# Sixteen more tokens by row gathers instead of dense experts, and squares of finished rows in SBUF

## Chip, core and metric

One core of a Trainium2 chip runs the whole program. The metric is device time in microseconds (us) of one execution; the kernel before takes 3629.07 us (median of three runs, 3625.85 to 3631.55). Engines are named as in the profile: PE is TensorE's matrix products and PEld its weight loads, DVE is VectorE, ACT is ScalarE, POOL is GpSimd, SP is SyncE, which issues most DMAs.

## What is computed

A decoder block on 512 tokens of width 2048 in float32: convolution and attention mixers (`w_in`, `w_mix`, `w_out`), then an expert layer. Each token chooses, for 8 heads, 16 of 16384 experts (a row of `u` and a row of `v` each), so 128 experts per token:

```
top_s, top_i = lax.top_k(scores, 16)            # per half of the key
sel_s, sel_pos = lax.top_k(cand_s, 16)          # of the 16 x 16 sums
gate = softmax(sel_s)
hidden = einsum("td,thkd->thk", x, u_table[sel_i])
act = gelu(hidden) * gate
out = einsum("thk,thkd->td", act, v_table[sel_i])
return rmsnorm(x + out, norm_final)
```

## The kernel before

The expert layer is done in two ways at once. Tokens 0 to 191 (`G0 = P + NG2`, NG2 = 64, lines 32 and 33) go by row gathers: an indirect DMA on POOL's queue fetches one expert row of 8 KB for each of 128 partitions (line 685, in `gather_tile`), and DVE multiplies it with the token (line 696, a sum per partition) or adds it, weighted, to the token's result (line 703). The other `ND` = 320 tokens go dense: PE multiplies them with all 16384 experts (`dense`), and planes of gates, zero for experts that a token did not choose, mask the activations (line 774).

A gather run keeps 128 partitions full. The first run has 128 tokens with 128 slots each (128 gathers of `u`, then 128 of `v`). The second has 64 tokens on two partition groups, each with 64 of the slots (64 and 64 gathers). At its end the second group's partial sums are moved over with a DMA and added (lines 757 and 758, in `finish`); then `finish_rows` (line 722) squares the rows on ACT for their norm (`rms_scale`, line 189, which writes the squares to a z tile in PSUM, line 193), scales them and stores them.

The dense part has 128 tiles of 128 experts in 16 chunks of 8. `up` makes 48 products per tile (16 blocks of the width, three products each, lines 164 to 166, since a float32 weight is split into a high part, line 133, and a low part, line 134). `down` makes as many for each pair of 128 output columns. So a unit is always 48 products of 128 x 128 weights with ND columns, and it reads 1 MB of weights in two halves (`whalf`, line 142, issue on line 148). There are 256 units: the ups of chunks 0 to 7 (units 0 to 63, while the routing of the later tokens and the gate planes are made beside them), the downs of chunks 0 to 7 (64 to 127), and then up and down of each chunk in turn. The activations of the first eight chunks go to memory without gates (`hdd`, line 800) and come back (`hb`, line 813); the gate planes come back from `gd` as `gt` (line 769). The tokens' products with z tiles in PSUM are added to `dacc` (line 838); in the last down the results are transposed (line 843), added to the residual (line 845), normalized and stored.

The order of each engine's instructions is fixed before the run from a simulated timeline. Gathers are called for by `pump`, once or more per unit: at fixed rates in the mixers and up to unit 59, afterwards at the rate that spreads what is left (`rounds`, line 904) over the units up to 246, times 0.9 below unit 128 (lines 1036 to 1039). A gather is held back by a dependency on a product's output of that time; its consumers on DVE stay in program order. Rows have 4 buffers of 1 MB. What is left of the gathers and the finish is called for between the last up and the last down (`"last"`).

Of the kernel before, what the change touches and what calls it, by code (L numbers as in the profile page):

```python
# [18 lines left out]
P = 128  # L19
# [12 lines left out]
NG2 = 64  # L32
# [48 lines left out]
def block_kernel(ctx, tc, a, out, dbg=None):  # L81
# [77 lines left out]
    def behind(ins):  # L159
        """Queue ins on its engine behind the latest weight product."""  # L160
        tc.add_manual_dep(ins.ins, pe_last[0].ins.name, mybir.DependencyInfo(mybir.DependencyClass.NoSync, mybir.DependencyReason.DATA), reason="behind")
# [27 lines left out]
    def rms_scale(pool, x):  # L189
        ss = pool.tile([P, 2], F32, name="ss", bufs=2)  # L190
        for c in range(2):
            junk = ztile()
            nc.scalar.activation(junk, x[:, c * 1024:c * 1024 + 1024], AF.Square, accum_out=ss[:, c:c + 1])  # L193
        return rms_inv(ss)

    def rms_inv(ss):
        nc.vector.tensor_tensor(ss[:, 0:1], ss[:, 0:1], ss[:, 1:2], OP.add)
        nc.scalar.activation(ss[:, 0:1], ss[:, 0:1], AF.Sqrt, scale=1.0 / D, bias=epst)
# [3 lines left out]
    def turn(x2, k, pin):  # L202
        """Two 128-column blocks of the pair of row tiles, transposed: [128, 2, 256]."""
# [9 lines left out]
    def load_x(h):  # L213
        """Transposed tokens of one half times the norm's gains, split; 1 / rms of each token to inv."""
# [46 lines left out]
    def mixer(h, st, x):  # L261
        """Attention, convolution and their gated merge for one half of the tokens; the merge goes to
        md, and the last of it straight to the tiles of the output projection."""
# [157 lines left out]
    def suffix(pool, z, sp, seg, nj, W):  # L421
        """z minus the sums of sp over the keys from each key to the end."""
# [22 lines left out]
    def outproj(pool, h, m, box):  # L445
        """Output projection and residual of 256 tokens."""
# [38 lines left out]
    def chain(pool, h, box, nhi, nlo, c0):  # L485
        """Normalized, transposed and split tokens of one half from column c0; tokens 0.. to xn2d."""
# [35 lines left out]
    def queries(pool, h, st, nhi, nlo, c0):  # L522
        """Product-key scores of 256 tokens, queued for the top 16 of each group."""
# [25 lines left out]
    def route(pool, tile_no, st):  # L549
        """Product-key routing of one 128-token tile: expert halves and gate of each slot."""  # L550
# [12 lines left out]
        # Of the 16 x 16 sums of two sorted lists only those with (a + 1) * (b + 1) <= 16 can be among  # L563
        # the first 16; rows a of widths 16, 8, 4, 1 hold them all, in the order of the full list.
# [16 lines left out]
        # Position in the compact list -> row a and column b.  # L581
# [52 lines left out]
    def gates(pool, eg, p0, b0, nb):  # L634
        """Dense gate planes of 16-token blocks b0.. from tokens on partitions p0.. of a routing tile."""
# [40 lines left out]
    def gather_tile(pool, np_, nslot, idx, gate, load_x, load_acc, finish):  # L676
        """Row gathers for np_ partitions of (token, slot group), nslot slots each."""
# [50 lines left out]
    def gather(routes):  # L728
        idx = routes[0][0]
        yield from gather_tile(  # L730
            late[1], P, P, idx, st["gate"],
            lambda t: nc.sync.dma_start(t, xn2d[0:P]),
            lambda t: nc.sync.dma_start(t, x2d[0:P]),
            lambda t: finish_rows(t, slice(0, P), final_gain()))
        if not NG2:
            return
        S = P // (P // NG2)
        idx, eg = routes[1]
        idx2 = late[1].tile([P, S], I32, name="idx2")
        gate2 = late[1].tile([P, S], F32, name="gate2")  # L740
        for r in range(P // NG2):
            ps_, ss = slice(r * NG2, r * NG2 + NG2), slice(r * S, r * S + S)
            nc.sync.dma_start(idx2[ps_], idx[0:NG2, ss])
            nc.sync.dma_start(gate2[ps_], eg[0:NG2, 2, ss])

        def load_x(t):
            for r in range(P // NG2):
                nc.sync.dma_start(t[r * NG2:r * NG2 + NG2], xn2d[P:G0])
# [339 lines left out]
```

## Time and profile before

| | us |
|---|---|
| median of the runs | 3629.07 |
| span of the profiled execution | 3629.1 |
| PE busy in it | 3535.7 |
| DVE busy | 2833.4 |
| ACT busy | 1621.6 |
| POOL busy | 644.8 |

The profiled execution's own time is its span; nothing of it lies outside, and it stands at the median of the runs. The page's rows of 40 slices show PE at 8 or 9 tenths in all of them and DVE at 5 to 9 tenths; the DMA engines are at 5 or 6 tenths in the first quarter, in which no gathers run, and at 7 to 9 tenths until the last slice. The core moved 1056.10 MB, 402.68 MB of it by the gathers' queue (q0) and 649.38 MB by SP's (q1).

### The profile page before, as it was taken

Reading aid. Unit: us, or ns where it says so; the run is one execution under the profiler, and the core shown is the slowest. Engines: PE = TensorE matmul, PEld = TensorE weight load, DVE = VectorE, ACT = ScalarE, POOL = GpSimd, SP = SyncE. Lnnn points to the kernel's source line nnn. Section 1 sums busy time; section 2 is a strip of 40 time slices with the busy share of each in tenths; the row PEclk is TensorE's granted clock in tenths of the full one; section 3 lists DMA queues with packets and bytes.
Section 4 is the critical chain, followed back from the end, with each engine's and each line's share of the span. In section 5 each row is a group of like instructions: output and inputs, shape, how many; then the busy total and the mean of one; then the engine's idle time right before and its main releaser. Section 6 shows DMA issues by size and latency. Waiting matters only on the chain.

```text
span 3629.1 us, 63343 instructions
## 1 busy us (share of the span) xinstructions
PE 3535.7 (97%) x25347; PEld 3420.6 (94%) x25347; DVE 2833.4 (78%) x4022; ACT 1621.6 (45%) x2277; POOL 644.8 (18%) x520
## 2 busy tenths in 40 slices
PE   9999999999999999889999999999999999999998
PEld 8999999798888999779999999999999999999997
DVE  6555557558988888788999886888887888888885
ACT  5444445445545543554337773333333333333334
POOL 0000000000234222012121111221122322322220
PEclk9999999999999999999999999999999999999998
DMA  5556666663788899899889889899988988889884
GB/s 194 170 176 219 214 216 216 198 193 127 267 306 332 335 344 356 313 331 344 295 324 334 309 317 364 326 358 337 341 328 327 358 328 336 325 338 349 326 319 150
DMA packets 297815, 1056.10 MB, mean 291 GB/s; under 512 B 36464, under 2 KB 109296, under 8 KB 243568
## 3 DMA queue, kind: packets, MB, share of 16 engines
q1 hardware_dynamic: 242224, 649.38, 51.3%
q0 software_dynamic: 55296, 402.68, 28.9%
q8 instruction: 199, 3.26, 0.3%
q14 instruction: 96, 0.79, 0.1%
HBM read 999.98 MB, written 51.38 MB: 290 GB/s over the span
## 4 chain that ended last, share of the span: by engine, by line
PE 73%; DVE 3%; DMA 2%; issue 2%; ACT 1%; POOL 0%; SPq 0%; DVEq 0%; ACTq 0%; POOLq 0%
PE pj L166 13%; PE pj L164 13%; PE pj L165 13%; PE z L164 9%; PE z L165 9%; PE z L166 9%; PE pj L668 2%; DVE wlo L134 1%; PE z L434 1%; PE tr L416 1%; DVE row L696 1%; DMA wraw<-in_w_mix 1%; DMA row<-in_u,idx 1%; PE z L397 0%; DMA gt<-gd 0%
## 5 line engine op out<-in xcount | busy, mean ns | idle before, releaser
L133 ACT ACTIVATE whi<-wraw 128x1024 fp32r<-128x1024 f32 x827 | 874.2, 1059 | 1229.3 <-PE pj L165 726.4
L134 DVE TENSOR_TENSOR wlo<-wraw,whi 128x1024 fp32r<-128x1024 f32 x827 | 1009.2, 1224 | 415.3 <-ACT whi L133 409.5
L166 PE MATMUL pj<-xhi,wlo 128*128 128x256 f32 x2560 | 719.7, 282 | 11.3 <-DVE wlo L134 11.1
L164 PE MATMUL pj<-xhi,whi 128*128 128x256 f32 x2560 | 721.6, 282 | 6.7 <-ACT whi L133 4.7
L165 PE MATMUL pj<-xlo,whi 128*128 128x256 f32 x2560 | 720.5, 282 | 0.0
L164 PE MATMUL pj<-dxhi,whi 128*128 128x320 f32 (+1 forms) x2304 | 710.0, 308 | 2.8 <-ACT whi L133 2.6
L166 PE MATMUL pj<-dxhi,wlo 128*128 128x320 f32 (+1 forms) x2304 | 704.1, 307 | 4.5 <-DVE wlo L134 4.5
L165 PE MATMUL pj<-dxlo,whi 128*128 128x320 f32 (+1 forms) x2304 | 705.8, 307 | 0.0
L164 PE MATMUL z<-ahi,whi 128*128 128x320 f32 x2048 | 631.0, 309 | 4.0 <-ACT z L193 2.9
L165 PE MATMUL z<-alo,whi 128*128 128x320 f32 x2048 | 631.5, 309 | 2.4 <-DVE alo L134 2.4
L166 PE MATMUL z<-ahi,wlo 128*128 128x320 f32 x2048 | 629.6, 309 | 1.8 <-DVE wlo L134 1.8
L166 PEld LDWEIGHTS pj<-xhi,wlo 128*128 128x128 f32 x2560 | 480.0, 188 | 21.5 <-DVE wlo L134 16.1
L164 PEld LDWEIGHTS pj<-xhi,whi 128*128 128x128 f32 x2560 | 481.7, 188 | 12.6 <-ACT whi L133 6.1
L165 PEld LDWEIGHTS pj<-xlo,whi 128*128 128x128 f32 x2560 | 481.4, 188 | 6.7 <-issue 5.3
L685 POOL DMA_INDIRECT row<-in_v,idx x192 | 286.7, 1493 | 1063.8 <-DVE row L703 448.9
L703 DVE SCALAR_TENSOR_TENSOR row<-row,gact 128x2048 f32<-128x2048 f32 x192 | 450.5, 2346 | 19.3 <-DMA row<-in_v,idx 19.3
L696 DVE SCALAR_TENSOR_TENSOR row<-row,gx 128x2048 f32<-128x2048 f32 x192 | 438.4, 2287 | 26.0 <-DMA row<-in_u,idx 25.0
L685 POOL DMA_INDIRECT row<-in_u,idx x192 | 290.8, 1515 | 857.8 <-DVE row L696 213.0
L166 PEld LDWEIGHTS pj<-dxhi,wlo 128*128 128x128 f32 x2304 | 433.3, 188 | 5.6 <-DVE wlo L134 5.6
L164 PEld LDWEIGHTS pj<-dxhi,whi 128*128 128x128 f32 x2304 | 434.5, 189 | 3.2 <-ACT whi L133 2.9
L165 PEld LDWEIGHTS pj<-dxlo,whi 128*128 128x128 f32 x2304 | 434.2, 188 | 0.0
L133 ACT ACTIVATE whi<-spare 128x1024 fp32r<-128x1024 f32 x197 | 208.8, 1060 | 414.8 <-PE z L165 263.8
(232 smaller groups left out, 5019.3 us busy)
## 6 DMA issues: line engine op xcount, KB each, us to landing
wraw<-in_w_in SPq DMA_DIRECT2D x320, 512.0 KB
wraw<-in_uT SPq DMA_DIRECT2D x187, 512.0 KB
wraw<-in_vT SPq DMA_DIRECT2D x128, 512.0 KB
spare<-in_vT SPq DMA_DIRECT2D x128, 512.0 KB
spare<-in_uT SPq DMA_DIRECT2D x69, 512.0 KB
wraw<-in_w_mix SPq DMA_DIRECT2D x64, 512.0 KB
wraw<-in_w_out SPq DMA_DIRECT2D x64, 512.0 KB
wraw<-in_wq SPq DMA_DIRECT2D x64, 512.0 KB
```

Source lines behind the costliest of these rows:

```text
L133: nc.scalar.activation(hi, src, AF.Copy)
L134: nc.vector.tensor_tensor(lo, src, hi.bitcast(F32), OP.subtract)
L164: nc.tensor.matmul(acc, shi, mhi, start=first, stop=False)
L165: nc.tensor.matmul(acc, shi, mlo, start=False, stop=False)
L166: pe_last[0] = nc.tensor.matmul(acc, slo, mhi, start=False, stop=last)
L416: nc.tensor.matmul(yps[hs, q0:], kv[j // 2][1][:, j % 2, hs], e[:, seg(j)], start=j == 0, stop=j == last, skip_group_check=True)
L434: nc.tensor.matmul(z[:, c], stat.bitcast(F32), src[:, c], start=False, stop=True, skip_group_check=True)
L668: behind(nc.tensor.matmul(gp[:, t * P:t * P + P], oh[:, t, 0], oh[:, t, 1], start=True, stop=True))
L685: ins = nc.gpsimd.indirect_dma_start(out=g, out_offset=None, in_=tab, in_offset=bass.IndirectOffsetOnAxis(ap=idx[0:np_, s:s + 1], axis=0))
L696: pin(nc.vector.scalar_tensor_tensor(g, g, 1.0, gx, OP.mult, OP.mult, accum_out=hid[:, s:s + 1]))
L703: pin(nc.vector.scalar_tensor_tensor(acc[0:np_], g, act[:, s:s + 1], acc[0:np_], OP.mult, OP.add))
```

## The change

NG2 becomes 80, so G0 is 208, ND is 304 and there are 19 gate-plane blocks of 16 tokens instead of 20. A list of runs takes the place of the two written-out ones: 128 tokens, 64 tokens on two slot groups, and then 16 tokens on eight slot groups with 16 gathers of `u` and 16 of `v`. The finish of a run adds the partial sums in halves: one move and one addition for the second run, three of each, one after the other, for the third. `rms_scale` squares in eight steps of 256 columns into an SBUF tile instead of two steps of 1024 into PSUM. `rounds` is 416 instead of 384; the rates stay.

```diff
-NG2 = 64
+
+SEGS = ((0, 0, 128), (1, 0, 64), (1, 64, 16))
+NG2 = 80
...
     def rms_scale(pool, x):
-        ss = pool.tile([P, 2], F32, name="ss", bufs=2)
-        for c in range(2):
-            junk = ztile()
-            nc.scalar.activation(junk, x[:, c * 1024:c * 1024 + 1024], AF.Square, accum_out=ss[:, c:c + 1])
-        return rms_inv(ss)
+        ss = pool.tile([P, 8], F32, name="ss", bufs=2)
+        for c in range(8):
+            junk = pool.tile([P, 256], F32, name="junk", bufs=1)
+            nc.scalar.activation(junk, x[:, c * 256:c * 256 + 256], AF.Square, accum_out=ss[:, c:c + 1])
+        nc.vector.tensor_reduce(ss[:, 0:1], ss, AX.X, OP.add)
+        return rms_root(ss)
...
+        for tile_no, p0, n in SEGS:
+            R = P // n
+            rows = slice(tile_no * P + p0, tile_no * P + p0 + n)
+            idx, eg = routes[tile_no]
+            gate = st["gate"]
+            if R > 1:
+                src, idx = idx, late[1].tile([P, n], I32, name=f"idx{n}")
+                gate = late[1].tile([P, n], F32, name=f"gate{n}")
+                for r in range(R):
+                    ps_, ss = slice(r * n, r * n + n), slice(r * n, r * n + n)
+                    nc.sync.dma_start(idx[ps_], src[p0:p0 + n, ss])
+                    nc.sync.dma_start(gate[ps_], eg[p0:p0 + n, 2, ss])
+
+            def load_x(t):
+                for r in range(R):
+                    nc.sync.dma_start(t[r * n:r * n + n], xn2d[rows])
+
+            def load_acc(t):
+                if R > 1:
+                    nc.vector.memset(t, 0.0)
+                nc.sync.dma_start(t[0:n], x2d[rows])
+
+            def finish(t):
+                m = P // 2
+                while m >= n:
+                    o = row()
+                    nc.sync.dma_start(o[0:m], t[m:2 * m])
+                    nc.vector.tensor_tensor(t[0:m], t[0:m], o[0:m], OP.add)
+                    m //= 2
+                finish_rows(t, rows, final_gain())
+
+            yield from gather_tile(late[1], P, n, idx, gate, load_x, load_acc, finish)
...
-    rounds = 2 * P + (2 * (P // (P // NG2)) if NG2 else 0)
+    rounds = sum(2 * n for _, _, n in SEGS)
```

## Rows read from the trace of the kernel before

**Rows 1.** Busy us and instructions per engine in stretches; then PEclk, DMA share, GB/s.
```profile
1350.00:1450.00 100.00, 98.38 (x826) 97.34 (x825) 82.97 (x87) 40.47 (x51) 23.43 (x15) 1.00 0.96 353
1716.40:1950.00 233.60, 230.22 (x1573) 229.42 (x1572) 228.89 (x555) 103.89 (x152) 47.41 (x31) 0.99 0.86 314
1950.00:2238.00 288.00, 283.66 (x2026) 282.87 (x2025) 230.29 (x446) 186.34 (x384) 43.36 (x33) 0.99 0.90 330
2238.00:2696.90 458.90, 453.61 (x3072) 450.48 (x3072) 391.03 (x369) 159.23 (x185) 91.93 (x65) 1.00 0.92 339
2697.10:3545.30 848.20, 845.33 (x5761) 844.64 (x5759) 695.48 (x632) 305.29 (x375) 221.41 (x136) 1.00 0.89 335
```

**Rows 2.** Start and us of single matmuls in the dense part (timeline, PE).
```profile
2999.81 0.31 PE L166 MATMUL z<-ahi,wlo 128*128 128x320 f32 x1
...
3003.63 0.31 PE L165 MATMUL z<-alo,whi 128*128 128x320 f32 x1
```

**Rows 3.** The same view in the second mixer, 256 columns.
```profile
1319.79 0.28 PE L164 MATMUL pj<-xhi,whi 128*128 128x256 f32 x1
...
1321.68 0.28 PE L166 MATMUL pj<-xhi,wlo 128*128 128x256 f32 x1
```

**Rows 4.** Gathers (line 685) in stretches: POOL's busy us and count, clock, DMA share.
```profile
900.00:1716.40 816.40, 173.40 (x119) 0.99 0.88 324
...
2238.00:2696.90 458.90, 91.93 (x65) 1.00 0.92 339
2697.10:3545.30 848.20, 221.41 (x136) 1.00 0.89 335
```

**Rows 5.** DMA queues from 2238.0 to 2696.9: packets, MB, share of 16 engines.
```profile
q1 hardware_dynamic: 45524, 86.79, 53.5%
q0 software_dynamic: 9360, 68.16, 37.7%
```

**Rows 6.** DMA queues from 2697.1 to 3545.3.
```profile
q1 hardware_dynamic: 53020, 139.19, 45.5%
q0 software_dynamic: 19728, 143.66, 42.8%
q8 instruction: 45, 0.74, 0.3%
```

**Rows 7.** Short full stretches: busy us per engine, PEclk, DMA share, GB/s.
```profile
2200.00:2250.00 50.00, 46.24 (x304) 45.72 (x303) 35.32 (x36) 18.16 (x26) 10.17 (x7) 0.97 1.00 374
...
3000.00:3010.00 10.00, 10.00 (x70) 10.00 (x70) 7.41 (x7) 2.75 (x3) 2.42 (x2) 1.00 0.99 391
```

**Rows 8.** SP's timeline, the last issue of a weight half.
```profile
3570.06 0.33 SPq L148 DMA_DIRECT2D spare<-in_vT  x1
```

**Rows 9.** ACT's timeline, the last split of a weight half.
```profile
3593.86 1.06 ACT L133 ACTIVATE whi<-wraw 128x1024 fp32r<-128x1024 f32 x1 [0.49 <-ACT hd L847]
```

**Rows 10.** Groups of instructions: busy us, mean ns; then idle before and releaser.
```profile
L703 DVE SCALAR_TENSOR_TENSOR row<-row,gact 128x2048 f32<-128x2048 f32 x192 | 450.5, 2346 | 19.3 <-DMA row<-in_v,idx 19.3
L696 DVE SCALAR_TENSOR_TENSOR row<-row,gx 128x2048 f32<-128x2048 f32 x192 | 438.4, 2287 | 26.0 <-DMA row<-in_u,idx 25.0 <-DVE wlo L134 1.0
L668 PE MATMUL pj<-spare 128*128 128x128 f32 x640 | 86.2, 275 | 0.6 <-DVE spare L651 0.6
```

**Rows 11.** PE's waits from 2690 to 2830: total us, times, longest.
```profile
PE z L164 <- ACT z L193: 2.9, 1, 2.9
```

**Rows 12.** SP's timeline at the finish of the second run.
```profile
3536.68 0.48 SPq L757 DMA_DIRECT2D row<-row  x1
...
3552.65 0.52 SPq L726 DMA_DIRECT2D out<-row  x1
...
3557.13 0.33 SPq L882 DMA_DIRECT2D row<-x2d  x1
```

**Rows 13.** DVE's timeline there and in the last down.
```profile
3542.09 2.28 DVE L758 TENSOR_TENSOR row<-row 64x2048 f32<-64x2048 f32 x1
...
3566.13 0.42 DVE L845 TENSOR_TENSOR row<-tr,row 128x256 f32<-128x256 f32 x1
```

More of the change, by code (lines that the diff above doesn't have):

```diff
@@ L189, in rms_scale, with rms_root @@
     def rms_scale(pool, x):
-        ss = pool.tile([P, 2], F32, name="ss", bufs=2)
-        for c in range(2):
-            junk = ztile()
-            nc.scalar.activation(junk, x[:, c * 1024:c * 1024 + 1024], AF.Square, accum_out=ss[:, c:c + 1])
-        return rms_inv(ss)
+        ss = pool.tile([P, 8], F32, name="ss", bufs=2)
[4 more added lines that the diff above has]
+        return rms_root(ss)
     def rms_inv(ss):
         nc.vector.tensor_tensor(ss[:, 0:1], ss[:, 0:1], ss[:, 1:2], OP.add)
+        return rms_root(ss)
+    def rms_root(ss):
         nc.scalar.activation(ss[:, 0:1], ss[:, 0:1], AF.Sqrt, scale=1.0 / D, bias=epst)
@@ L728, in gather @@
     def gather(routes):
[L729 to L748, printed above, removed]
-        def load_acc(t):
-            nc.vector.memset(t, 0.0)
-            nc.sync.dma_start(t[0:NG2], x2d[P:G0])
-        def finish(t):
-            for r in range(1, P // NG2):
-                o = row()
-                nc.sync.dma_start(o[0:NG2], t[r * NG2:r * NG2 + NG2])
-                nc.vector.tensor_tensor(t[0:NG2], t[0:NG2], o[0:NG2], OP.add)
-            finish_rows(t, slice(P, G0), final_gain())
@@ L761, in gather @@
-        yield from gather_tile(late[1], P // NG2 * NG2, S, idx2, gate2, load_x, load_acc, finish)
+        for tile_no, p0, n in SEGS:
[26 more added lines that the diff above has]
+            yield from gather_tile(late[1], P, n, idx, gate, load_x, load_acc, finish)
```

## The prediction

> **What bounds the kernel now.** I read the busy shares by stretch first. From unit 64 on (2238 us) PE is busy 453.6 of 458.9 us and then 845.3 of 848.2 us, its clock fully granted, while the DMA engines are at 0.92 and 0.89 and DVE at 85% and 82% [rows 1]. So PE sets the pace there, and DMA is close behind. In the first quarter of the dense part (1716.4 to 1950) PE is busy 230.2 of 233.6 us, but DVE is busy 228.9: the routing of the later tokens lies there, and DVE is as full as PE. Next is what PE's busy time consists of. Two dense matmuls 26 steps apart begin at 2999.81 and 3003.63 [rows 2]: 147 ns a step; with 256 columns 16 steps take 1.89 us, 118 ns [rows 3]. The count in 848.2 us (5761, 147 ns) says the same. The step depends on the columns: (146.5 - 118.1) / 64 = 0.44 ns a column, so 16 columns fewer give 7.1 ns. I take this slope although it is drawn between two points only, since 304 lies between them.
>
> **What PE saves.** A unit is 48 matmuls: 48 x 7.1 ns = 0.341 us, 7.03 to 6.69 us. 256 units give 87.3 us. This is the ceiling; the rest is what prevents it.
>
> The Trainium skill (TensorE: Matmul & The Clock Gate, Back-to-back issue gap) has a sustained spacing of about 81 ns at 128 columns and 131 ns at 512, which is 0.13 ns a column; by it, as an estimate, the ceiling would be 12288 x 2.1 ns = 26 us instead of 87. The rows differ, in level and in slope, and I go by the rows.
>
> **What the gathers add.** `pump` is unchanged until unit 59. 119 gathers are issued before the dense part [rows 4] and one a unit follows, so 178 are called by then. Of 386 calls 208 were left; now 240 of 418 are. By the formula (0.9 of the even rate, then the even rate) a share of (118/187)^0.9 = 0.66 of that is left at unit 128: 137 before, where the trace has 136 [rows 4], and 159 now. So of the 32 new gathers 10.6 fall into units 64 to 127 and 21.2 into the stretch from 2697.1 to 3545.3.
>
> Price of one in DMA time: 37.7% of 458.9 us over 65 gathers is 2.66 us of all 16 engines [rows 4, 5], and 42.8% of 848.2 us over 136 is 2.67 us [rows 4, 6]. What shrinks by a twentieth is the activations read back and the gate planes: about 18 MB in the first of these stretches, 9 MB in the second (from the tiles' sizes), at 2.8 us a MB of SP's queue [rows 5, 6]: 2.5 and 1.3 us off. The third run loads its token rows once more (1 MB, 2.9 us).
>
> DMA time of units 64 to 127: (53.5 + 37.7 + 0.3)% of 458.9 = 419.9 us [rows 5], with the 0.3 of instruction loads taken from [rows 6], + 28.2 - 2.5 = 445.6 us. PE needs 458.9 - 21.8 = 437.1 us. Stretch to 3545.3: 88.6% of 848.2 = 751.5 [rows 6], + 56.6 - 1.3 + 2.9 = 809.7 us. PE needs 848.2 - 120 x 0.341 = 807.3 us. So DMA becomes as long as PE in both: **this is the step on which the result hangs**. What share can the DMA engines sustain? In 1350 to 1450 they held 0.96 while PE was busy 98.4 of 100 us [rows 1]: lower end. They are at 1.00 over 50 us at 2200 and at 0.99 at 3000, with PE full in the latter [rows 7]: upper end. Weight halves come early in the dense part (the last is issued at 3570.06 and the last split begins at 3593.86, 24 us [rows 8, 9]), which lets DMA run without gaps when it is the later one. I take 0.985, somewhat nearer to the full end for that cushion: 445.6/0.985 = 452.4 us, **6.5 us gained**, and 809.7/0.985 = 822.0 us, **26.2 us gained**. At 0.96: -5.3 and +4.8. At 1.00: +13.3 and +38.5.
>
> **The other stretches.** Units 0 to 31 (1716.4 to 1950): DVE has 228.9 us of work that does not shrink, and 233.6 - 228.9 = 4.7 us is all there is unless work moves later. I take 3 (0 to 10.9, PE's saving). Units 32 to 63 (1950 to 2238): DVE 80%, DMA 0.90, gathers at the old rate; all of PE's 32 x 0.341 = 10.9. Last down, 8 units without gathers: 2.7.
>
> **DVE's share of the gathers.** Each costs 2.29 us (and a read of the sum) or 2.35 us [rows 10]. In the late stretch 21.2 x 2.4 = 51 us and about 11 us of the third finish come to 695.5: 757 of 822 us, 92%. This is hidden as long as DVE stays under PE; if it were not, it would cost what is over. POOL's issues (221 us for 136 in 848 us, [rows 4]) have room for 21 more.
>
> **Squares in SBUF.** PE waited once for a z tile that squares held, 2.9 us [rows 11]; gone, 2.9 us gained (0 to 2.9, since another wait may end there). Eight squares with their sum's read take longer on ACT than two; ACT is at 36% in that stretch [rows 1].
>
> **Gate planes of the mixers.** 16 tokens less of 320: 32 of 640 small matmuls of 0.275 us or less a step [rows 10], in a part whose end PE does not always set: 1 us (0 to 8.8).
>
> **SP's queue.** 16 more loads of slot indices and gates, 8 more of token rows, each about 0.5 us of issue (0.48 in [rows 12]). Queued behind them are weight halves, which have spare time in the dense part, less in the mixers, where the index loads can go as soon as routing is done: -1 us (0 to -9).
>
> **The tail.** The second run's finish now lies in the middle, beside products; the third comes last. Before, from the move at 3536.68 over the addition (3542.09 + 2.28) one round takes 7.7 us, and stores go at 3552.65 [rows 12, 13]. Two more rounds, smaller moves, are at most 15 us, eight squares some 2.5 more. Behind this wait the rows into which the residuals of the last down are loaded: the last at 3557.13 is needed at 3566.13 [rows 12, 13]. So its addition can be some 10 us late, and weight splits stand behind it on DVE, three halves ahead of PE (10 us). Cost 0 to 15, nothing below zero, as no work of the end goes away; I take 5, for the cushion covers most.
>
> **Sum.** 3 + 10.9 + 6.5 + 26.2 + 2.7 + 2.9 + 1 - 1 - 5 = 47.2 us off the span of 3629.1, which stands at the median: **3582 us**. With DMA at 0.96 3615, at 1.00 3563.
>
> **Rivals.**
> - PE stays the bound everywhere: packets move faster when queues are full. For it: 391 GB/s at 3000 [rows 7], where the late stretch would need 306 MB (283.6 + 22.2, the token rows, less half a MB) in 807 us, 380 GB/s. Against it: 374 GB/s at a full share over 50 us, with PE down to 46.2 [rows 7]. 87.3 + 2.9 - 5 = 85 us off: 3544 us, 3539 with no cost at the tail.
> - **Slower: DMA cannot hold its share.** The place is units 64 to 248; both stretches together need 445.6 + 809.7 = 1255 us of DMA. The rest of the sum is worth 14.5 us, so all gain is gone where 1255/s = 1307.1 + 14.5, at s = 0.95. It decides from there: DVE then waits for rows in a fixed order (45 us of such waits already, [rows 10]), splits stand behind it and PE stops. Halfway between the 0.92 of units 64 to 127 and the 0.96 of the mixers [rows 1], 0.94, the time is 1335 us: 13.8 us over, 3643 us. Against it: in those units PE was still the bound, so 0.92 shows no limit.
> - In bytes, both stretches will need 472 MB; the point of no gain is 472 MB / 1321.6 us = 357 GB/s, and both are at 335 to 339 now [rows 1]. If a steady rate near that is the limit, the time stays at 3629 us. The Trainium skill (DMA: Bandwidth & Descriptors, Where 436 GB/s comes from) holds HBM's share of a core, about 358 GB/s, to bind for loads from HBM; as an estimate by that figure 1318 us and a total of 3626. The rows show 374 and 391 GB/s on one active core, over 50 and 10 us, so it is no hard cap here.
> - The change doesn't do what it says: a floor of the weight loads keeps the step at 146.5 ns. Then only the tail and the z wait are left, 3631 us. The 118 ns at 256 columns speak against it [rows 3].
>
> **How the numbers follow.** The forecast (DMA-bound between 0.96 and 1.00, 3563 to 3615) has 0.50, PE-bound (3539 to 3563) 0.19, a rate or share about the point of no gain, or no saving on PE (3615 to 3636) 0.18, slower than that 0.13. Differences under 0.2% (7.3 us) can hardly be told from no change. Faster by more than that, below 3621.8: the first two and a part of the third, 0.76; within 0.12; slower 0.12. The range leaves out a tenth on each side: 3543 to 3637.
>
> **What will show it.** The step of dense matmuls should be 139 to 140 ns. PE's share from 2238 on should fall below 0.99 with the DMA share at 0.97 or more; PE's waits there should be for weight halves (splits), and DVE's for gathered rows. If the DMA share is under 0.95 and PE is full, the second case holds; if the DMA share is under 0.95 and PE is not full, my price of sharing is wrong. In 1716 to 1950 little should change. The last transposes should wait for residual rows. The sum is wrong if gathers pile up before unit 64, or if the new fixed order of instructions moves work between stretches.

## The result, and the profile after

The changed kernel takes 3718.43 us (median of four runs, 3712.51 to 3723.24), the kernel before 3630.31 us beside it (four runs). The ratio is 1.0235, 95% interval 1.0215 to 1.0255: **2.35% slower**, where 1.3% faster was forecast and 3637 us was the range's upper end. The profiled execution has a span of 3714.8 us, 85.7 more than the span of before.

The page's engine row and its rows of 40 slices say where to look: PE is at 8 or 9 tenths, as before, in every slice but the last two, where it falls to 4 tenths and 1 and its granted clock to 7 tenths and 5.

```profile
PE 3471.9 (93%) x25315; PEld 3343.1 (90%) x25315; DVE 2901.6 (78%) x4054; ACT 1625.1 (44%) x2301; POOL 673.2 (18%) x552
...
PE   9999999999999999989989999999999999999941
...
PEclk9999999999999999999999999999999999999975
DMA  5556666654788999889888899999999899989884
```

Stretches of the changed kernel, busy us of each engine with instructions, then PEclk, DMA share, GB/s. They are units 64 to 127, the units up to the last up, the last down, and everything behind the last dense matmul:

```profile
2234.00:2687.00 453.00, 438.01 (x3073) 432.53 (x3072) 395.41 (x372) 158.16 (x185) 96.77 (x69) 0.99 0.95 351
2687.00:3516.00 829.00, 813.78 (x5763) 809.89 (x5762) 685.74 (x630) 309.23 (x398) 190.46 (x135) 0.99 0.91 341
3516.00:3570.00 54.00, 53.77 (x387) 53.52 (x386) 49.52 (x49) 19.60 (x25) 18.57 (x12) 1.00 0.83 316
3570.00:3715.00 145.00, 15.88 (x50) 5.97 (x48) 81.22 (x92) 21.98 (x73) 31.16 (x19) 0.52 0.55 195
```

The first two rows answer to the last two of [rows 1]: 453 for 458.9 us and 829 for 848.2 us. The dense part ends at 3570.2 us; before, it ended at 3604.9, 24.2 us ahead of the end of the program. So **PE's part gained 34.7 us, and what lies behind it grew from 24.2 to 144.6 us, by 120.4**; 120.4 - 34.7 = 85.7, the whole difference.

The products got shorter as forecast. 22 steps of the late stretch take 3.07 us, 139.5 ns each, where 26 of the kernel before take 147 each [rows 2]:

```profile
2995.80 0.30 PE L166 MATMUL z<-ahi,whi 128*128 128x304 f32 x1
...
2998.87 0.30 PE L167 MATMUL z<-alo,whi 128*128 128x304 f32 x1
```

The last of the stretches tells what the 145 us are: POOL still issues gathers in them, and PE works for 16 us. Single instructions there, of several engines (start, us, engine, line, operation; in brackets the idle time before and what ended it):

```profile
3570.21 0.30 PE L168 MATMUL z<-ahi,wlo 128*128 128x304 f32 x1
...
3631.15 0.94 POOL L691 DMA_INDIRECT row<-in_v,idx  x1 [3.06 <-DVE row L709]
...
3635.53 4.82 DVE L709 SCALAR_TENSOR_TENSOR row<-row,gact 128x2048 f32<-128x2048 f32 x2 [1.29 <-DMA row<-in_v,idx]
...
3640.37 12.35 SPq L763 DMA_DIRECT2D row<-row  x3
...
3644.57 2.28 DVE L764 TENSOR_TENSOR row<-row 64x2048 f32<-64x2048 f32 x1 [4.22 <-DMA row<-row]
3649.88 2.28 DVE L764 TENSOR_TENSOR row<-row 32x2048 f32<-32x2048 f32 x1 [3.03 <-DMA row<-row]
3655.60 2.28 DVE L764 TENSOR_TENSOR row<-row 16x2048 f32<-16x2048 f32 x1 [3.44 <-DMA row<-row]
...
3664.04 2.35 DVE L731 SCALAR_TENSOR_TENSOR row<-row,ss 128x2048 f32<-128x2048 f32 x1
3666.31 0.41 DVE L852 TENSOR_TENSOR row<-tr,row 48x256 f32<-48x256 f32 x1
...
3666.85 2.60 SPq L889 DMA_DIRECT2D row<-x2d  x2
...
3672.08 0.42 DVE L852 TENSOR_TENSOR row<-tr,row 128x256 f32<-128x256 f32 x1 [4.37 <-DMA row<-x2d]
```

Read downwards: the last gather is issued at 3631.15 and the last gathered row is added by 3640.35 (70.1 us behind the dense part); then comes the third run's finish in its three rounds, with squares and scaling, until 3666.3 (26 us). Only then do two of the three residual rows of the last down start to load, the last one at 3666.85 or later where before it went at 3557.13 [rows 12], and the 24 pairs of transposes with their additions take most of the remaining 48.5 us. PE's own longest wait says it in one line (waits of PE: total us, times, longest):

```profile
PE tr L850 <- DVE row L852: 117.7, 23, 96.3
```

Why gathers are left over is in the count and in what POOL waited for. POOL's gathers in stretches of the changed kernel (length, busy us and count, then clock, DMA share, GB/s):

```profile
900.00:1716.80 816.80, 171.44 (x119) 0.98 0.87 322
1716.80:2234.00 517.20, 99.74 (x63) 0.98 0.88 322
2234.00:2687.00 453.00, 96.77 (x69) 0.99 0.95 351
2687.00:3516.00 829.00, 190.46 (x135) 0.99 0.91 341
```

119, and 63 where the same view of before counts 64; then 69 and 135, where the prediction had 76 and 157. With 416 in all, 30 were left at the end of the last up; before, none. The late stretch issues one gather per 6.14 us now and issued one per 6.24 us before [rows 4]: calling for more did not serve more.

POOL's longest waits ahead of gathers, over the whole span of the changed kernel (total us, times, longest):

```profile
POOL row L691 <- DVE row L709: 661.1, 126, 15.5
POOL row L691 <- DVE row L702: 433.1, 85, 24.6
POOL row L691 <- issue: 135.8, 70, 11.5
```

and of the kernel before:

```profile
POOL row L685 <- DVE row L703: 448.9, 91, 14.0
POOL row L685 <- DVE dacc L838: 321.4, 42, 15.7
POOL row L685 <- DVE row L696: 213.0, 33, 25.0
```

Two kinds of wait stand here. `DVE dacc L838` is the addition of a product's output: POOL waits for the time at which `pump` calls the gather. `DVE row L703` is the multiply-add that reads a gathered row: POOL waits for a free buffer. Before, the first kind was 321.4 us, which looks like room, but 448.9 us of the second kind were there already. After, the first kind is gone from the top of the list, and the second has grown to 661.1 us. The limit moved from the call to the buffer.

The cycle of a buffer can be read from two timelines of the changed kernel, POOL's and, below it, DVE's line 709:

```profile
3383.44 1.68 POOL L691 DMA_INDIRECT row<-in_v,idx  x1 [5.78 <-DVE row L709]
...
3403.60 0.94 POOL L691 DMA_INDIRECT row<-in_v,idx  x1 [5.04 <-DVE row L709]
...
3380.82 2.35 DVE L709 SCALAR_TENSOR_TENSOR row<-row,gact 128x2048 f32<-128x2048 f32 x1
3387.54 2.35 DVE L709 SCALAR_TENSOR_TENSOR row<-row,gact 128x2048 f32<-128x2048 f32 x1
3394.26 2.35 DVE L709 SCALAR_TENSOR_TENSOR row<-row,gact 128x2048 f32<-128x2048 f32 x1
3400.98 2.35 DVE L709 SCALAR_TENSOR_TENSOR row<-row,gact 128x2048 f32<-128x2048 f32 x1
```

In a `v` phase one of the four row buffers is the running result, so three carry gathers. The gather issued at 3383.44 (as soon as 3380.82 + 2.35 had freed a buffer) is read three places later, at 3400.98, and its buffer is issued into again at 3403.60: 20.2 us a turn here, for a transfer that takes 8.1 us (median of this stretch's `v` gathers). Three buffers in 20.2 us are one gather per 6.7 us; the whole late stretch, in which `u` phases with all four buffers are half of the gathers, has one per 6.14. The call needed 829/157 = 5.3.

Of this turn the transfer takes 8.1 us and the multiply-add 2.35; the rest, about half, is mostly the wait for the row's place in DVE's order, between the work for the products. Behind the dense part, where that work is gone, the same three buffers serve 16 `v` gathers in 55.7 us, one per 3.7, with transfers of 7.4 us (median). Three times 3.7 is a turn of 11 us:

```profile
L691 POOL DMA_INDIRECT row<-in_v,idx x16: 932/940/3052, 3575.4 to 3631.1; - x16
```

So the limit is the number of buffers together with how long the order on DVE holds each.

### The profile page after: what moved, and what is told of

It reads as the page before. It is cut to its first block, busy times and chain, and to the rows that moved or that the text cites. A ratio compares the mean times of both kernels' runs of the same rounds, so it can differ in the third digit from the quotient of the medians.

```text
span 3714.8 us, 63459 instructions
## 1 busy us (share of the span) xinstructions
PE 3471.9 (93%) x25315; PEld 3343.1 (90%) x25315; DVE 2901.6 (78%) x4054; ACT 1625.1 (44%) x2301; POOL 673.2 (18%) x552
## 5 line engine op out<-in xcount | busy, mean ns | idle before, releaser
L166 PE MATMUL pj<-dxhi,whi 128*128 128x304 f32 (+1 forms) x2304 | 699.8, 304 | 7.5 <-ACT whi L135 5.6
L168 PE MATMUL pj<-dxhi,wlo 128*128 128x304 f32 (+1 forms) x2304 | 692.9, 302 | 5.7 <-DVE wlo L136 5.6
L167 PE MATMUL pj<-dxlo,whi 128*128 128x304 f32 (+1 forms) x2304 | 694.9, 302 | 0.0
L168 PE MATMUL z<-ahi,wlo 128*128 128x304 f32 x2048 | 618.7, 304 | 15.1 <-DVE wlo L136 15.1
L166 PE MATMUL z<-ahi,whi 128*128 128x304 f32 x2048 | 620.7, 304 | 12.0 <-ACT ahi L135 8.8
L167 PE MATMUL z<-alo,whi 128*128 128x304 f32 x2048 | 622.2, 304 | 1.4 <-DVE alo L136 1.4
L709 DVE SCALAR_TENSOR_TENSOR row<-row,gact 128x2048 f32<-128x2048 f32 x208 | 487.9, 2346 | 60.8 <-DMA row<-in_v,idx 58.5
L702 DVE SCALAR_TENSOR_TENSOR row<-row,gx 128x2048 f32<-128x2048 f32 x208 | 475.0, 2287 | 45.2 <-DMA row<-in_u,idx 44.8
L691 POOL DMA_INDIRECT row<-in_v,idx x208 | 308.0, 1481 | 1103.3 <-DVE row L709 631.0
L168 PEld LDWEIGHTS pj<-xhi,wlo 128*128 128x128 f32 x2560 | 479.1, 188 | 20.0 <-DVE wlo L136 14.5
L168 PEld LDWEIGHTS z<-ahi,wlo 128*128 128x128 f32 x2048 | 387.0, 189 | 17.4 <-DVE wlo L136 17.3
```

Source lines behind the costliest of these rows:

```text
L166: nc.tensor.matmul(acc, shi, mhi, start=first, stop=False)
L167: nc.tensor.matmul(acc, shi, mlo, start=False, stop=False)
L168: pe_last[0] = nc.tensor.matmul(acc, slo, mhi, start=False, stop=last)
L691: ins = nc.gpsimd.indirect_dma_start(out=g, out_offset=None, in_=tab, in_offset=bass.IndirectOffsetOnAxis(ap=idx[0:np_, s:s + 1], axis=0))
L702: pin(nc.vector.scalar_tensor_tensor(g, g, 1.0, gx, OP.mult, OP.mult, accum_out=hid[:, s:s + 1]))
L709: pin(nc.vector.scalar_tensor_tensor(acc[0:np_], g, act[:, s:s + 1], acc[0:np_], OP.mult, OP.add))
```

## The experiments

Each kernel was timed beside the kernel before on its chip; ratios are to that. Diffs are against the changed kernel unless said otherwise.

### What stops the gathers

**One gather buffer more in the `v` phases.** The running result goes to the tile that held the token's row during the `u` phase, so that all four row buffers carry gathers.

```diff
-                acc = row()
+                acc = late[1].tile([P, D], F32, name="gx", bufs=1)
```

> The changed kernel, but the running result of a gather run stands in the tile of the token rows (free once the products with u are done) and no longer in one of the 4 row buffers, so 4 instead of 3 buffers carry gathers in the v phases. Theory A, the row buffers limit the gathers (in the v phases a gather is issued 0.3 us after the third row before it is consumed, one per 6.3 us, while 5.0 to 5.5 us are called for): one gather per 5.0 to 5.6 us from 2250 us on, the last one issued before 3560 us, total 3570 to 3610 us. Theory B, the bandwidth of the DMA engines limits them: the spacing stays at 6.0 us or more and the total within 1% of 3718 us. Theory C, the calls of the last units come too late: total stays too, since the calls don't move.

3688.10 us, 1.0142 (1.0125 to 1.0159). Between 3200 and 3300 us, in a `v` phase, this kernel issues 20 gathers (the view of line 691: count, then shortest, median and longest in ns, first and last start):

```profile
L691 POOL DMA_INDIRECT row<-in_v,idx x20: 936/1676/3201, 3199.2 to 3299.0; - x20
```

The changed kernel issues 16 in the same view:

```profile
L691 POOL DMA_INDIRECT row<-in_v,idx x16: 937/1586/1682, 3202.7 to 3299.9; - x16
```

No gather is left to issue behind the dense part, so the row buffers, at the time each is held, were the limit. The whole late stretch has 148 gathers in 852 us, one per 5.8. The time is 78 us above the upper end that I expected, for two reasons. The finish and the residual rows still follow the last gather closely (issued 3610.3): 75 us lie behind the dense part, since the tile that now holds the result can take the third run's token rows only when the second run is done (POOL stands still for 28.5 us at 3452). And the dense part itself ends at 3618.6, 48.4 us later than in the changed kernel:

```profile
2232.00:2706.00 474.00, 448.04 (x3074) 440.23 (x3073) 411.39 (x380) 158.50 (x187) 128.97 (x73) 0.97 0.93 349
2706.00:3558.00 852.00, 824.08 (x5763) 816.77 (x5762) 710.11 (x659) 313.95 (x406) 232.30 (x148) 0.99 0.93 348
```

These are its units 64 to 127 and the units up to the last up, columns as above; 474 and 852 us are no shorter than before the change, with products that are 5% shorter. With the 24.2 us behind the dense part that the kernel before has, the sum would be 3643 us.

**Calls earlier, consumers earlier.** Two ways in which the calls or the place of the consumers could be to blame: the last gathers called 40 units ahead of the end instead of 10, and the multiply on DVE put into the order one gather earlier.

```diff
-DRAIN = 10
+DRAIN = 40
```

> The changed kernel with the last gather called for 40 instead of 10 units before the end (unit 216 instead of 246), everything else the same. Theory A: a gather waits for a row buffer and not for its call (165 us behind its call at 3500 us), so the total stays between 3700 and 3725 us. Theory C (calls come too late): the tail of 145 us after the last dense matmul shrinks to under 50 us, total under 3630 us.

3715.24 us, 1.022 (1.020 to 1.024): no change. POOL's wait for line 709 is 657.1 us, as in the changed kernel. The calls are not late; they are not served.

```diff
-DEPTH = 1
+DEPTH = 0
```

> The changed kernel with a gathered row's DVE product called for in the same step as its gather and not one step later (DEPTH 0 instead of 1). In the changed kernel a row is held 17 us in the median from issue to consumption, though it lands after about 8. Theory A (row buffers, held too long by the order on DVE, limit the gathers): held 10 to 13 us, one gather per 5.0 to 5.5 us, tail under 60 us, total 3590 to 3640 us. Theory B (DMA bandwidth or DVE limit the dense part once gathers keep up): the gathers keep up but PE loses as much, the dense matmuls end after 3610 us, total over 3660 us. If the order on DVE is set by other work: holding time and total as in the changed kernel, 3700 to 3725 us.

3722.78 us, 1.0233 (1.0160 to 1.0307): no change either. The multiply-adds stand where they stood (3380.53, 3387.25, 3393.97, 3400.69), one per 6.72 us. So this constant does not set how long a row waits. That the simulated timeline sets it, in which the three buffers are taken too, is inferred.

**More gathers ahead of unit 60.** The rate up to unit 59 is 1.4 a unit instead of 1.

```diff
-RATE_W = 1.0
+RATE_W = 1.4
```

> The changed kernel with 1.4 instead of 1 gather called for per unit in units 0 to 59, where one is issued per 8 us and rows are free: 24 gathers move there from the stretch in which the row buffers limit them. Theory A: the last gather is issued about 24 x 6 = 140 us earlier, near 3490 us plus what the early stretch loses; that stretch loses 5 to 40 us, since DVE was full in its first half and 24 x 2.35 us are added; total 3600 to 3650 us. If not the number of gathers behind unit 60 but the shape of the last run sets the tail (its transition and its finish): over 3680 us.

3689.20 us, 1.0141 (1.0108 to 1.0175). 81 instead of 63 gathers go into the first 64 units. Two gathers are read behind the dense part instead of some 20, but this part ends at 3603.3, 33 us later: units 0 to 63 alone take 556 us instead of 517. Neither range that I expected holds 3689 us: the backlog is gone as in theory A, but the early stretch lost its price there. With the end of the kernel before the sum would be 3627 us, no better than before.

**The small run in the middle.** Runs of 128, 16 and 64 tokens instead of 128, 64 and 16, so that the finish with three rounds lies beside products.

```diff
-SEGS = ((0, 0, 128), (1, 0, 64), (1, 64, 16))
+SEGS = ((0, 0, 128), (1, 64, 16), (1, 0, 64))
```

> The changed kernel with its runs in the order 128, 16, 64 tokens: the same number of gathers, the small run and its three rounds of partial sums beside products and the one-round finish of the run of 64 at the end. Theory A (the number of gathers against the row buffers): as many gathers left at the end of the dense part, total 3690 to 3720 us, some 10 us less than the changed kernel for two rounds of the finish. Theory D (the small run itself is what costs, being last): total under 3660 us.

3718.43 us, 1.0222 (1.0188 to 1.0255): no change, and the 10 us less for two rounds of the finish can't be seen either. 135 us lie behind the dense part, with gathers in them until 3643.4. Which run comes last hardly matters; that gathers come last does.

### What the rest of the change does

**The gathers alone.** The kernel before with its 320 dense columns and squares in PSUM; the third run is added, and serves tokens that the second one serves too, so 16 tokens are done twice. Against the kernel before:

```diff
-    rounds = 2 * P + (2 * (P // (P // NG2)) if NG2 else 0)
+    rounds = sum(2 * n for _, _, n in SEGS)
...
+SEGS = ((0, 0, 128), (1, 0, 64), (1, 48, 16))
```

> The kernel before (320 dense tokens, squares in PSUM) with a third run of 16 tokens on eight slot groups that does tokens 176 to 191 a second time: 32 more gathers and no faster matmuls. Theory A: the gathers keep their spacing of about 6.2 us, fall behind as in the changed kernel, and about 30 are left at the end of the dense part (3605 us): total 3720 to 3770 us. Theory B: the DMA engines have room here (a unit lasts 7.03 us and not 6.69), the gathers are hidden: under 3660 us.

3758.45 us, 1.0339 (1.0318 to 1.0360). So the 32 gathers and their finish cost 123.5 us where PE saves nothing. PE's longest wait there shows that a part of it goes by way of the squares:

```profile
PE z L166 <- ACT z L195: 103.1, 2, 78.3
```

The squares of the last run hold a z tile, which stands in the fixed order ahead of the last down's products, and wait for the last gathers: PE stands for 78.3 us.

This kernel also tells what holds the rows. From 3340 to 3440 us PE works for only 42 us, and 23 `v` gathers are issued (busy us of PE, PEld, DVE, ACT and POOL), with three buffers as ever: where the products stand, rows are read sooner.

```profile
3340.00:3440.00 100.00, 42.26 (x289) 41.99 (x287) 73.94 (x45) 14.27 (x15) 41.22 (x23) 0.72 0.86 319
```

**Squares in PSUM.** The change without its second part.

```diff
-        ss = pool.tile([P, 8], F32, name="ss", bufs=2)
-        for c in range(8):
-            junk = pool.tile([P, 256], F32, name="junk", bufs=1)
-            nc.scalar.activation(junk, x[:, c * 256:c * 256 + 256], AF.Square, accum_out=ss[:, c:c + 1])
...
+        ss = pool.tile([P, 2], F32, name="ss", bufs=2)
+        for c in range(2):
+            junk = ztile()
+            nc.scalar.activation(junk, x[:, c * 1024:c * 1024 + 1024], AF.Square, accum_out=ss[:, c:c + 1])
```

> The changed kernel with the squares of finished rows in a z tile of PSUM again, in two steps of 1024. My price for this part was 2.9 us: 3710 to 3725 us. The other view: where the finish is late, the products of the last down wait for the z tile of its squares, as they did for 78 us in the run with gathers alone, so the last down (54 us) starts only after the last finish (3664 us) and the total is 3735 to 3770 us.

3733.50 us, 1.0263 (1.0223 to 1.0303). That is 15 us above the changed kernel, but on a chip on which the kernel before took 9 us more as well; by the ratios (1.0235 there, with overlapping intervals) no difference is clear, and the time lies between the two ranges that I expected. PE waits 124.8 us for such z tiles, 96.0 at once, and the dense part ends at 3711.1 instead of 3570.2. Most of that wait only changes its place, since the last transposes wait for the gathers anyway.

**Squares in SBUF alone**, put into the kernel before (with four buffers instead of five for the activations, to make room). Against the kernel before:

```diff
-HBB = 5
+HBB = 4
...
-        ss = pool.tile([P, 2], F32, name="ss", bufs=2)
-        for c in range(2):
-            junk = ztile()
...
+        ss = pool.tile([P, 8], F32, name="ss", bufs=2)
+        for c in range(8):
+            junk = pool.tile([P, 256], F32, name="junk", bufs=1)
```

> The kernel before with the squares of finished rows in SBUF in eight steps, and nothing else of the change (one buffer less for activations that come back, to make room). Price of the prediction: 2.9 us gained, so 3625 to 3637 us beside 3630 to 3640 of the kernel before: no difference that can be told. If the z tile mattered at the end of the kernel before as it does in the changed one, over 15 us are gained.

3636.50 us, 1.0004 (0.9992 to 1.0016): no difference. So of my 2.9 us nothing can be told, and that the tile is worth more once gathers are late is not shown.

### What PE gains, and what takes it

**Without the third run.** The changed kernel with 304 dense columns, and tokens 192 to 207 computed nowhere.

```diff
-SEGS = ((0, 0, 128), (1, 0, 64), (1, 64, 16))
+SEGS = ((0, 0, 128), (1, 0, 64))
```

> The changed kernel without its third run: tokens 192 to 207 get no experts and aren't stored. Gathers are 384 as before, the dense part has 304 columns. Theory A: the gather stream is as long as in the kernel before (its last gather issued near 3500 to 3530 us), the dense matmuls end near 3520 to 3540, total 3540 to 3570 us. If the step of 139.5 ns or the price of the dense part were misjudged: over 3590 us. If the squares or the new runs' code cost something by themselves: above the dense end by more than 40 us.

3606.13 us, 0.9920 (0.9900 to 0.9940). This is what the 16 columns give with no gather more: 28.8 us of the ceiling's 87, and the time is above the 3590 us that I had set for a misjudged dense part. The dense part ends 36 us earlier than before, at 3568.5, but the second run's rows are stored no earlier (3553.41 for 3552.65 [rows 12]), so 36.8 us lie behind it for 24.2: with shorter products the gathers of before end too late already. The stretches of the dense part:

```profile
2240.00:2685.00 445.00, 433.48 (x3074) 429.20 (x3074) 387.78 (x369) 158.17 (x185) 99.40 (x66) 1.00 0.94 350
2685.00:3514.00 829.00, 813.42 (x5762) 811.03 (x5761) 682.29 (x629) 306.04 (x386) 209.26 (x137) 0.99 0.90 338
```

829 us in the late one although the gathers are as many as before (137 for 136) and the DMA share is only 0.90. PE needs 807 us there by the prediction's own figure.

Where do the 22 us go? PE stands still nine times, 17.1 us in all. Six of these waits, 14.5 us, look like this one (ACT's timeline, then DVE's, then PE's):

```profile
2868.88 1.06 ACT L135 ACTIVATE whi<-spare 128x1024 fp32r<-128x1024 f32 x1 [2.29 <-PE z L167]
...
2875.72 0.79 DVE L845 TENSOR_TENSOR dacc<-z,dacc 128x608 f32<-128x608 f32 x1 [3.70 <-PE z L168]
2876.42 2.28 DVE L702 SCALAR_TENSOR_TENSOR row<-row,gx 128x2048 f32<-128x2048 f32 x1
...
2878.63 1.22 DVE L136 TENSOR_TENSOR wlo<-spare,whi 128x1024 fp32r<-128x1024 f32 x1
...
2879.90 0.41 PE L168 MATMUL z<-ahi,wlo 128*128 128x304 f32 x1 [3.95 <-DVE wlo L136]
...
2882.55 0.46 PE L166 MATMUL z<-ahi,whi 128*128 128x304 f32 x1
2882.80 0.46 PE L167 MATMUL z<-alo,whi 128*128 128x304 f32 x1
```

ACT had split this weight half by 2869.94, so it had landed before. DVE could have made the low part (line 136) then, but the fixed order has the addition to `dacc` ahead of it, which waits for PE's last product of the unit, and a gathered row behind that. So DVE idles for 3.70 us, waiting for PE, and then PE for 3.95, waiting for DVE. In all six, ACT's split had ended 4 to 8 us before PE stopped. In this stretch an addition to `dacc` stands ahead of the split that PE needs next 6 times out of 57, and 6 times in the changed kernel too (13.6 of its 17.1 us of waits); in the kernel before, never.

Most of the rest is the clock. After this wait the granted clock is 0.50 from 2881.0 to 2884.3, the lower of its two levels (1.2 of 2.4 GHz), and products begin 0.25 us apart instead of 0.14. About 14 us of the late stretch go by at that level, which costs some 6 us.

**Half the bytes.** To see whether the DMA load takes the difference, three kernels gather half rows: 4 KB for each partition instead of 8, so the results are those of other rows. The `u` product is then two DVE instructions. The rest of the program text is as it was, but the order of each engine's instructions comes anew from the simulated timeline. The first is the kernel before with this edit, a control; the second is the one without the third run; the third has the third run and the result in the other tile.

```diff
-            ins = nc.gpsimd.indirect_dma_start(out=g, out_offset=None, in_=tab, in_offset=bass.IndirectOffsetOnAxis(ap=idx[0:np_, s:s + 1], axis=0))
+            ins = nc.gpsimd.indirect_dma_start(out=g[:, 0:D // 2], out_offset=None, in_=tab.rearrange("e (h d) -> (e h) d", h=2), in_offset=bass.IndirectOffsetOnAxis(ap=idx[0:np_, s:s + 1], axis=0))
...
-                pin(nc.vector.scalar_tensor_tensor(g, g, 1.0, gx, OP.mult, OP.mult, accum_out=hid[:, s:s + 1]))
+                for c in range(2):
+                    pin(nc.vector.scalar_tensor_tensor(g[:, 0:D // 2], g[:, 0:D // 2], 1.0, gx[:, c * 1024:c * 1024 + 1024], OP.mult, OP.mult, accum_out=hid[:, s:s + 1]))
...
-            pin(nc.vector.scalar_tensor_tensor(acc[0:np_], g, act[:, s:s + 1], acc[0:np_], OP.mult, OP.add))
+            gg = g[:, 0:D // 2].unsqueeze(1).broadcast_to([np_, 2, D // 2])
+            ac = acc[0:np_].rearrange("p (h d) -> p h d", h=2)
+            pin(nc.vector.scalar_tensor_tensor(ac, gg, act[:, s:s + 1], ac, OP.mult, OP.add))
```

> The kernel before with gathers of 4 KB instead of 8 KB a row (the wrong half rows; DVE still works through 2048 columns, so its time stays): the control for the next two. PE sets its pace, so the dense matmuls can gain what PE lost there, 5 to 15 us of 1888; total 3600 to 3635 us, DMA share in the last dense stretch about 0.68 instead of 0.89.

> The changed kernel without its third run (tokens 192 to 207 get no experts) and with gathers of 4 KB (wrong half rows), to be compared with the control. With full rows the dense matmuls ended 36 us earlier than in the kernel before, and 87 us were worked out from the columns. If the DMA engines held the rest back: the dense part ends 70 to 90 us earlier than in the control, total 3520 to 3550 us. If DVE or the fixed order of instructions holds it: 30 to 50 us earlier, total 3570 to 3595 us.

> The changed kernel with the running result out of the row buffers, as in the first run, and gathers of 4 KB (wrong half rows). In that run gathers kept up and the dense matmuls ended at 3618 us, 48 us later than in the changed kernel, with DMA at 0.93. If the DMA engines are what slows PE once the gathers keep up: dense end 3530 to 3560, total 3570 to 3620 us. If it is DVE's order (87% and 83% busy): dense end after 3590, total over 3650 us.

The control takes 3667.38 us, 1.0090 (1.0061 to 1.0119): not faster, as I had expected, but slower: its dense part begins 21 us later, and units 64 to 127 take 471 us at a DMA share of 0.75, 12 more than before. I put this down to the second DVE instruction for a row, which no run tests by itself. The late stretch is 849.5 us, as before. Without the third run it is 3567.52 us, 0.9815 (0.9787 to 0.9844); with it 3599.60, 0.9904 (0.9871 to 0.9936). The late stretch of the second kernel:

```profile
2679.30:3487.00 807.70, 805.76 (x5759) 804.77 (x5758) 693.64 (x759) 304.43 (x389) 223.24 (x137) 1.00 0.77 261
```

807.7 us: here PE gets what the prediction said that it needs (807.3). The whole dense part takes 1820.5 us, 84.4 less than the control's 1904.9, against a ceiling of 87.3. That control is a slow one, though; beside the kernel before (1888.5) it is 68. With full rows the same 16 columns gave 39 us (1849.1). So **what takes the rest goes away, for the most part, with half of the gathers' bytes**. The total of 3567.5 lies between the two ranges that I expected.

That the load on the DMA engines makes PE wait on the chip does not follow, as the edit changes the fixed order too. In the half-row kernel, as in its control, no addition to `dacc` of the late stretch stands ahead of the split that PE needs next. PE's waits for DVE's split in the down products are (with full rows and no third run, then with half rows; total us, times, longest):

```profile
PE z L168 <- DVE wlo L136: 10.9, 5, 4.0
...
PE z L168 <- DVE wlo L136: 1.9, 4, 0.8
```

Weights do land later under full rows: in the late stretch a half of `u` weights lands after 6.2 to 6.3 us (no third run) and after 4.2 to 4.5 us with half rows; for `v` weights it is 6.9 to 7.0 and 3.8 to 4.2. But in the kernel without the third run no wait for a weight half is among ACT's seven longest (the seventh is 2.0 us), and in the changed kernel, where its splits wait 26.0 us for halves, only some 3 us of PE's 17.1 follow from that (from 3123 to 3130). So most of what PE lost in these two kernels is the order on DVE, and the clock after it; with the fourth buffer it is half, 15.9 of 31.8 us. Whether the simulated timeline chose that order because of the longer transfers in it was not tested; a kernel with full rows and the order of the half-row kernel would tell.

With the third run, the half rows end the dense part at 3562.1, 56.5 us earlier than the same kernel with full rows, and leave 33 us behind it: the gathers keep up (last one issued 3484.6). The total is in the range that I expected for a limit by the DMA engines, the end of the dense part 2 us above it; as the order changed here too, this doesn't decide for that reading.

## Why the prediction was wrong, point by point

- **The step of PE: right.** A step takes 139.5 ns (result section), for 139.4. With half rows and no third run the late stretch came down to 807.7 us, for 807.3.
- **"How the gathers add": this step failed.** It took a gather that is called for as issued, and spread 32 more over units 64 to 247 by `pump`'s formula. Called they were; but in the `v` phases three buffers at 19 to 20 us a turn give one gather per 6.5 to 6.7 us, and the late stretch as a whole had the rate that the kernel before had already, so 30 were left at the end of the last up. I read POOL's busy time (221 us of 848) and called it room for 21 more. The room is not in the busy time. It is in what the idle time waits for: the page of before puts the largest part of the idle time ahead of the `v` gathers (448.9 of 1063.8 us) down to the DVE instruction that frees a row, and I used only the gathers' busy time. Even the waits for calls, 321.4 us, were not room: after the change 13.0 us are left of them, yet units 64 to the last up serve 204 gathers for 201 before, in nearly the same time.
- **The tail: -5 us, bound 15; measured 120.4.** Of this, 70 us are gathers behind the dense part, 26 the finish and 48.5 the transposes, less the 24.2 that were there before. The finish itself was sized well: from the first move to the store it takes 26.1 us (3640.37 to 3666.42) where the second run's took 16.0 (3536.68 to 3552.65 in [rows 12]), 10 more for the 17.5 that I allowed at most. But I had priced it as a delay of residual rows that a cushion covers. The cushion belonged to a finish that lies beside products. Once gathers come last, everything behind them lies bare.
- **DMA's share: the wrong limit.** I let PE run until the DMA engines are at 0.985. PE lost time earlier: 829 us at 0.90 (no third run), 852 at 0.93 (all gathers served), 808 at 0.77, for the same products. This is the case that the prediction named, "the DMA share is under 0.95 and PE is not full, my price of sharing is wrong". What the traces show in its place is DVE's fixed order, 14.5 of 17.1 us of PE's waits without the third run, and the lower clock after waits. The prediction had named a new fixed order as a way to fail, but put no price on it.
- **The rival "DMA cannot hold its share" came near in number.** It had a break-even at 0.95 and 1335 us for units 64 to 247; the kernel with the fourth gather buffer takes 1326, at 0.93. Its mechanism, DVE waiting for rows, is not what these traces show: in the late stretches DVE's longest waits are for ACT's split and for PE's last product. In bytes the rival had the point of no gain at 357 GB/s; that kernel has 348 to 349 there.
- **The argument against that rival was weak.** I said that 0.92 shows no limit, because PE was the bound. That PE is full tells nothing of how much shorter its products may become.
- **Units 64 to 127: 5.9 us gained, forecast 6.5; late 19.2, forecast 26.2; last down 5.3 for 2.7.** The first two are near, but for the wrong reason, as they hold 7 and 22 gathers fewer than I put there. Units 0 to 63 gained 4.2 us of 13.9: the first four chunks take 242.3 us for 240.7, where DVE is full [rows 1], and the next four 275.1 for 280.9. These are single profiles: in three kernels in which only calls or the order of runs differ the dense part ends at 3577 to 3584, for 3570.2, so some us either way mean little.
- **Squares: 2.9 us, not told apart from nothing** in the kernel before (1.0004), and with late gathers no clear difference either (1.0263 for 1.0235).
- **The Trainium skill's rules.** By the spacing that the Trainium skill gives (TensorE: Matmul & The Clock Gate, Back-to-back issue gap) the ceiling would have been 26 us, 2.1 ns for 16 columns; the steps above and in [rows 2] differ by 7.4 ns, so the rows decide. The Trainium skill's HBM share of 358 GB/s (DMA: Bandwidth & Descriptors, Where 436 GB/s comes from) gave a rival of 3626 us. Long stretches with full rows stay at 335 to 356 GB/s, and short ones went over it [rows 7]. No run here tests that limit by itself: with half rows the bytes, the landing times and the order on DVE all change.

**What stays open.** A fifth row buffer wasn't tried. That the simulated timeline holds a row for most of its 20 us is inferred: from the constant that changed nothing, the extra buffer that helped, and the turn of 11 us where no products stand between. No run changed DVE's order alone, neither to read rows sooner nor to bring the splits ahead of the additions; this is the test to make next. Why units 0 to 31 gain nothing is read only from DVE's fullness there [rows 1]. Of the kernels that compute everything, none beats the kernel before.

## What to carry to other kernels

Work that is moved from a full engine to a stream of requests is served at the stream's rate, not at the rate at which it is called: buffers divided by the time one is held, from issue to the last reader. Before adding requests, split the issuing engine's idle time into "waits for its call" and "waits for a buffer": the second is no room at all, and here even the first was not. What doesn't fit comes out at the end, with everything that is queued behind it. And when an engine's steps get shorter, look at the order of the engines that feed it, not only at the share of the transfers: one addition that waits for the end of a unit, placed ahead of the next unit's split, costs a stop and a slower clock after it.

## What the runs showed of the hardware

- Additions on 64, 32 and 16 partitions of 2048 columns all take 2.28 us (line 764, above): halving the rows in each round of the finish saves nothing on DVE.
- A weight half of 512 KB lands after 3.8 to 4.5 us where the DMA share is 0.77 and after 5.1 to 7.7 us at 0.90 to 0.91 (medians by stretch): the landing time rises before the engines are full.
- After a wait of PE of 3.95 us the granted clock stood at 0.50 for about 3 us of full work, and steps took 0.25 us for 0.14 (without the third run, 2881 to 2884). Over whole dense stretches above it was 0.97 to 1.00, and 0.52 in the 145 us in which PE mostly waits; each pair of transposes there takes 0.62 to 0.69 us.
